# SwiGLU on a 256 MiB input: groups of four rows per partition, whole 64 KiB stores

## Chip, cores and metric

The kernel runs on one core of a Trainium2 chip. The metric is device time in microseconds (us), lower is better. Before the change it is 935.98 us, the median of 3 runs (935.96 to 936.5).

## The reference

```python
def reference(x):                       # x: float32 [8192, 8192]
    a, b = np.split(x, 2, axis=-1)
    silu_b = b / (1 + np.exp(-b))
    return a * silu_b                   # float32 [8192, 4096]
```

Each row of 8192 numbers has its `a` in the first half and its `b` in the second. The input has 268.44 MB, the output 134.22 MB; each number is read or written once, and there is one activation and one product for each output.

## The kernel before, in words

All data stays float32. The 128 partitions of the on-chip memory (SBUF) each take `R = 2` neighbouring rows, so that a tile is 256 rows: 64 KiB in a row of each partition, 8.39 MB in all, and there are 32 tiles. Three slots of 64 KiB per partition (line 39) hold tile i in slot i modulo 3.

The work on a tile is four steps, each in place:

- `load` (line 54): one DMA from `x` into the slot, issued on SyncE's queue (SP). In the view `xv` the two rows of a partition are contiguous, so one partition's share is one piece of 64 KiB, and the whole tile is one contiguous stretch of the input.
- the gate (line 66): ScalarE (ACT) replaces the two `b` halves by their SiLU.
- the product (line 70): VectorE (DVE) multiplies `a` by the gate and packs the two products into the first 32 KiB of the slot's partition.
- `store` (line 75): one DMA of these 32 KiB per partition to `out`. Its queue is ACT's, for odd tiles 3 to 23 GpSimd's (POOL), and for the last two tiles SP's.

The order is written by hand: the program runs under `manual_schedule`, so each engine executes in the order of the loop from line 87. Waits come from the data, and `follows_from_others` (line 44) declares which of them are already implied. What matters for the change: load i+3 goes into the slot of tile i and waits for the store of tile i; it stands on SP right after that tile (line 104). Three loads are issued ahead (line 85).

The ends are cut finer: tiles 0, 1 and 2 compute row by row (`swiglu(i, k, k + 1)`), the first store goes out as 4 KiB and 28 KiB per partition (lines 91 and 92), the last load comes in two halves of 32 KiB per partition (lines 106 and 107), and the last tile is computed as one row and two half rows and is stored in two halves (lines 109 to 112).

Of the kernel before, what the change touches and what calls it, by code (L numbers as in the profile page):

```python
# [1 line left out]

# [4 lines left out]

_SILU = mybir.ActivationFunctionType.Silu


@with_exitstack
def kernel(
    ctx: ExitStack,
    tc: tile.TileContext,
    x: bass.AP,
    out: bass.AP,
):

    nc = tc.nc
    N, M = x.shape
    half = M // 2
    P = nc.NUM_PARTITIONS
    R = 2
    BUFS = 3  # L30

    xv = x.tensor.reshape([N // R, R * M]).ap()
    ov = out.tensor.reshape([N // R, R * half]).ap()
    ntiles = N // (P * R)
    last = ntiles - 1

    pool = ctx.enter_context(tc.tile_pool(name="sbuf", bufs=1))
    ctx.enter_context(tc.manual_schedule())
    slots = [pool.tile([P, R * M], x.dtype, name=f"slot{s}") for s in range(BUFS)]
    loads, gates, prods, stores = ([[] for _ in range(ntiles)] for _ in range(4))  # L40

    newest = {}

    def follows_from_others(inst, i, current, earlier):


        targets = [t for kind in current for t in kind[i]]
        targets += [t for kind in earlier for j in range(i % BUFS, i, BUFS) for t in kind[j]]
        for t in targets:
            if t is not newest.get(inst.ins.engine):  # L50
                tc.declare_no_dep(inst.ins, t.ins, reason="ordered by the other waits")
        newest[inst.ins.engine] = inst

    def load(i, c0=0, cw=R * M):
        inst = nc.sync.dma_start(  # L55
            out=slots[i % BUFS][:, c0 : c0 + cw], in_=xv[i * P : (i + 1) * P, c0 : c0 + cw]
        )
        follows_from_others(inst, i, [], [loads, gates, prods])
        loads[i].append(inst)

    def swiglu(i, k0=0, k1=R, c0=0, cw=half, gated=None):
        rows = slots[i % BUFS].rearrange("p (k s c) -> p k s c", k=R, s=2)
        a = rows[:, k0:k1, 0, c0 : c0 + cw]
        b = rows[:, k0:k1, 1, c0 : c0 + cw]
        o = slots[i % BUFS][:, : R * half].rearrange("p (k c) -> p k c", k=R)
        gate = nc.scalar.activation(out=b, in_=b, func=_SILU)  # L66
        follows_from_others(gate, i, [], [loads, gates, prods, stores])
        if gated:
            gated()
        prod = nc.vector.tensor_mul(out=o[:, k0:k1, c0 : c0 + cw], in0=a, in1=b)  # L70
        follows_from_others(prod, i, [loads], [loads, gates, prods, stores])
        gates[i].append(gate)
        prods[i].append(prod)

    def store(i, c0=0, cw=R * half):
        eng = nc.scalar if i < last - 1 else nc.sync
        if i % 2 and BUFS <= i < ntiles * 3 // 4:
            eng = nc.gpsimd
        inst = eng.dma_start(  # L79
            out=ov[i * P : (i + 1) * P, c0 : c0 + cw], in_=slots[i % BUFS][:, c0 : c0 + cw]  # L80
        )
        follows_from_others(inst, i, [loads, gates], [loads, gates, prods, stores])
        stores[i].append(inst)

    for i in range(BUFS):
        load(i)
    for i in range(last):
        if i == 0:

            swiglu(i, 0, 1)  # L90
            swiglu(i, 1, 2, gated=lambda: store(0, 0, half // 4))
            store(i, half // 4, R * half - half // 4)
        elif i < BUFS:
            for k in range(R):
                swiglu(i, k, k + 1)
            store(i)
        else:
            swiglu(i)
            if i == last - 1:
                swiglu(last, 0, 1)  # L100
            store(i)
        nxt = i + BUFS
        if nxt < last:
            load(nxt)
        elif nxt == last:
            load(last, 0, M)
            load(last, M, M)

    store(last, 0, half)
    for c0 in range(0, half, half // 2):  # L110
        swiglu(last, 1, 2, c0, half // 2)
    store(last, half, half)


# [1 line left out]
_INS = ['x']  # L116
_OUTS = [((8192, 4096), 'float32')]


# [23 lines left out]
```

## Time and profile before

| What | Value |
|---|---|
| Median of 3 runs | 935.98 us |
| Span of the profiled execution (first to last instruction) | 934.2 us |
| VectorE busy | 278.8 us, 30% of the span |
| ScalarE busy | 226.8 us, 24% |
| DMA: bytes and mean rate | 402.67 MB, 431 GB/s |
| Share of the DMA engines' time: SP's queue, ACT's, POOL's | 68.6%, 19.8%, 11.4% |
| A gate and a product of 128 x 8192 outputs | 7.03 us, 8.69 us |
| A gate and a product of 128 x 4096 outputs | 3.61 us, 4.43 us |
| Load, issue to landing (median of 31) | 38.4 us |
| Store of 4096 KB on ACT's queue, issue to landing (median) | 32.8 us |

Busy time of an engine counts its instructions alone, not the issue of DMAs. "Issue to landing" runs from the instruction that starts a transfer to the moment its semaphore is complete, so it holds the time in which the transfer shares the 16 DMA engines with others. The 40 slices of the page give the busy share of each engine in tenths over time; the chain gives the sequence of steps that ended last.

### The profile page before, as it was taken

Reading aid. Unit: us, or ns where it says so; the run is one execution under the profiler, and the core shown is the slowest. Engines: PE = TensorE matmul, PEld = TensorE weight load, DVE = VectorE, ACT = ScalarE, POOL = GpSimd, SP = SyncE. Lnnn points to the kernel's source line nnn. Section 1 sums busy time; section 2 is a strip of 40 time slices with the busy share of each in tenths; the row PEclk is TensorE's granted clock in tenths of the full one; section 3 lists DMA queues with packets and bytes.
Section 4 is the critical chain, followed back from the end, with each engine's and each line's share of the span. In section 5 each row is a group of like instructions: output and inputs, shape, how many; then the busy total and the mean of one; then the engine's idle time right before and its main releaser. Section 6 shows DMA issues by size and latency. Waiting matters only on the chain.

```text
span 934.2 us, 219 instructions
## 1 busy us (share of the span) xinstructions
DVE 278.8 (30%) x37; ACT 226.8 (24%) x38; POOL 6.2 (1%) x15
## 2 busy tenths in 40 slices
DVE  0333123332133321333213333133331233312342
ACT  0412320333202333023330233311333113331141
POOL 0000000000000000000000000000000000000000
DMA  9999999999999999999999999999999999999998
GB/s 404 418 426 434 427 441 450 432 427 429 446 414 441 428 443 431 428 434 459 429 413 460 410 446 428 428 446 427 428 429 464 408 429 446 428 446 428 427 428 382
DMA packets 9649, 402.67 MB, mean 431 GB/s; under 512 B 1072, under 2 KB 1072, under 8 KB 1200
## 3 DMA queue, kind: packets, MB, share of 16 engines
q1 hardware_dynamic: 5184, 276.83, 68.6%
q10 hardware_dynamic: 2880, 79.69, 19.8%
q0 software_dynamic: 1584, 46.14, 11.4%
q14 instruction: 1, 0.01, 0.0%
HBM read 268.44 MB, written 134.22 MB: 431 GB/s over the span
## 4 chain that ended last, share of the span: by engine, by line
DMA 70%; issue 12%; DVE 9%; ACT 7%; DVEq 0%; POOL 0%; SPq 0%; POOLq 0%
DMA slot<-in_x_dram 38%; DMA out_dram<-slot 32%; DVE slot L70 9%; ACT slot L66 7%; DVEq L138 0%; POOL out_dram L79 0%; SPq L55 0%; POOLq L79 0%; DVEq L70 0%
## 5 line engine op out<-in xcount | busy, mean ns | idle before, releaser
L70 DVE TENSOR_TENSOR slot<-slot 128x8192 f32<-128x8192 f32 (+2 forms) x37 | 278.8, 7539 | 641.5 <-ACT slot L66 641.2
L66 ACT ACTIVATE slot<-slot 128x8192 f32<-128x8192 f32 (+2 forms) x37 | 225.5, 6105 | 690.1 <-DMA slot<-in_x_dram 690.1
L79 POOL DMA_DIRECT2D out_dram<-slot x11 | 6.0, 544 | 695.6 <-DVE slot L70 695.6
L66 ACT ACT_TABLE_LOAD x1 | 1.3, 1283 | 0.7 <-PEq L127 0.7
L127 POOL MEMSET const-bfloat16-1.0<- 128x1 bf16 x1 | 0.1, 102 | 0.0
L127 POOL MEMSET const-float32-0.0<- 128x1 f32 x1 | 0.1, 99 | 0.2 <-issue 0.2
L127 POOL MEMSET const-float32-1.0<- 128x1 f32 x1 | 0.1, 99 | 0.0
L127 POOL MEMSET const-uint8-127<- 128x1 uint8 x1 | 0.1, 99 | 0.0
## 6 DMA issues: line engine op xcount, KB each, us to landing
out_dram<-slot ACTq DMA_DIRECT2D x18, 4096.0 KB, 32.8
out_dram<-slot POOLq DMA_DIRECT2D x11, 4096.0 KB, 32.6
slot<-in_x_dram SPq DMA_DIRECT2D x2, 4096.0 KB, 29.8
out_dram<-slot SPq DMA_DIRECT2D x1, 4096.0 KB, 19.3
out_dram<-slot SPq DMA_DIRECT2D x2, 2048.0 KB, 14.5
out_dram<-slot ACTq DMA_DIRECT2D x1, 3584.0 KB, 37.5
out_dram<-slot ACTq DMA_DIRECT2D x1, 512.0 KB, 24.6
slot<-in_x_dram SPq DMA_DIRECT2D x31, 38.4
```

What stands on the lines that cost most here:

```text
L66: gate = nc.scalar.activation(out=b, in_=b, func=_SILU)
L70: prod = nc.vector.tensor_mul(out=o[:, k0:k1, c0 : c0 + cw], in0=a, in1=b)
L79: inst = eng.dma_start(out=ov[i * P : (i + 1) * P, c0 : c0 + cw], in_=slots[i % BUFS][:, c0 : c0 + cw])
L127: nc = _bacc.Bacc("TRN2", target_bir_lowering=False, num_devices=1)
```

## The change

A partition now takes four neighbouring rows (`R = 4`): a group of 512 rows, 128 KiB of input and 64 KiB of output per partition, 16 groups in all. The memory is the same 3 x 64 KiB: two slots called `pack`, used by turns, and one called `extra`.

- The first two rows of a group are loaded into `pack` (h = 0), the last two into `extra` (h = 1). Each load still has 64 KiB per partition, but in `x` each partition's piece now lies 128 KiB from the next partition's.
- The products of `pack`'s two rows are written in place into its first 32 KiB; those of `extra`'s rows into the second 32 KiB of `pack`, whose inputs have been used up by then.
- The store sends the whole `pack`: 64 KiB per partition, one DMA, in ACT's queue, for the last two groups in SP's. The GpSimd queue isn't used.
- The load of `extra` for group g+1 waits for the last product of group g; the load of `pack` for group g+2 waits for the store of group g. They stand on SP in this order.
- The first rows of a group are computed in one gate and one product of 128 x 8192, the last two row by row, in two gates and two products of 128 x 4096.
- The finer cuts at the start and at the end are gone.

The functions `load`, `swiglu` and `store` after the change, and the loop:

```diff
-    R = 2
-    BUFS = 3
+    R = 4
+    W = R * half
...
-    slots = [pool.tile([P, R * M], x.dtype, name=f"slot{s}") for s in range(BUFS)]
+    packs = [pool.tile([P, W], x.dtype, name=f"pack{s}") for s in range(2)]
+    extra = pool.tile([P, W], x.dtype, name="extra")
...
+    def load(eng, g, h, *after):
+        tile_ = extra if h else packs[g % 2]
+        return ordered(
+            eng.dma_start(out=tile_, in_=xv[g * P : (g + 1) * P, h * W : (h + 1) * W]), *after
+        )
...
+    def swiglu(g, h, k0, k1, *after, behind=()):
+        rows = (extra if h else packs[g % 2]).rearrange("p (k s c) -> p k s c", k=2, s=2)
+        o = packs[g % 2].rearrange("p (h k c) -> p h k c", h=2, k=2)
+        b = rows[:, k0:k1, 1, :]
+        gate = ordered(nc.scalar.activation(out=b, in_=b, func=_SILU), *after)
+        return ordered(
+            nc.vector.tensor_mul(out=o[:, h, k0:k1, :], in0=rows[:, k0:k1, 0, :], in1=b),
+            gate, *behind,
         )
...
+    def store(eng, g, c0, c1, *after):
+        return ordered(
+            eng.dma_start(out=ov[g * P : (g + 1) * P, c0:c1], in_=packs[g % 2][:, c0:c1]), *after
+        )
...
-    for i in range(BUFS):
-        load(i)
-    for i in range(last):
...
+    first = {0: load(nc.sync, 0, 0)}
+    second = {0: load(nc.sync, 0, 1)}
+    first[1] = load(nc.sync, 1, 0)
+    for g in range(G):
+        prod = swiglu(g, 0, 0, 2, first[g])
+        prod = swiglu(g, 1, 0, 1, second[g], behind=[prod])
+        prod = swiglu(g, 1, 1, 2, behind=[prod])
+        if g < last:
+            second[g + 1] = load(nc.sync, g + 1, 1, prod)
+        stored = store(nc.sync if g >= last - 1 else nc.scalar, g, 0, W, prod)
+        if g + 2 < G:
+            first[g + 2] = load(nc.sync, g + 2, 0, stored)
```

`ordered` records each instruction and keeps, as its waits, the ones given to it and the order of its own engine.

More of the change, by code (lines that the diff above doesn't have):

```diff
@@ L28 @@
     P = nc.NUM_PARTITIONS
-    R = 2
-    BUFS = 3
+    R = 4
+    W = R * half
     xv = x.tensor.reshape([N // R, R * M]).ap()
-    ov = out.tensor.reshape([N // R, R * half]).ap()
-    ntiles = N // (P * R)
-    last = ntiles - 1
+    ov = out.tensor.reshape([N // R, W]).ap()
+    G = N // (P * R)
+    last = G - 1
     pool = ctx.enter_context(tc.tile_pool(name="sbuf", bufs=1))
     ctx.enter_context(tc.manual_schedule())
-    slots = [pool.tile([P, R * M], x.dtype, name=f"slot{s}") for s in range(BUFS)]
@@ L40 @@
[L40 to L50, printed above, removed]
-                tc.declare_no_dep(inst.ins, t.ins, reason="ordered by the other waits")
-        newest[inst.ins.engine] = inst
@@ L54, in load @@
-    def load(i, c0=0, cw=R * M):
-        inst = nc.sync.dma_start(
-            out=slots[i % BUFS][:, c0 : c0 + cw], in_=xv[i * P : (i + 1) * P, c0 : c0 + cw]
-        )
[L58 to L80, printed above, removed]
-        )
-        follows_from_others(inst, i, [loads, gates], [loads, gates, prods, stores])
-        stores[i].append(inst)
-    for i in range(BUFS):
-        load(i)
-    for i in range(last):
[L88 to L112, printed above, removed]
+    packs = [pool.tile([P, W], x.dtype, name=f"pack{s}") for s in range(2)]
+    extra = pool.tile([P, W], x.dtype, name="extra")
+    ops = []
+    def ordered(inst, *after):
+        before = [t for t in reversed(ops) if t.ins.engine == inst.ins.engine][:1]
+        for t in ops:
+            if not any(t is k for k in [*after, *before]):
+                tc.declare_no_dep(inst.ins, t.ins, reason="ordered by the other waits")
+        ops.append(inst)
+        return inst
```

## The prediction

> **What bounds the kernel now.** I read the page's 40 slices first, then the stretches, then the waits, the forms, the chain and the packet records.
>
> ```profile
> span 934.2 us, 219 instructions
> DVE 278.8 (30%) x37; ACT 226.8 (24%) x38; POOL 6.2 (1%) x15
> DMA  9999999999999999999999999999999999999998
> DMA packets 9649, 402.67 MB, mean 431 GB/s; under 512 B 1072, under 2 KB 1072, under 8 KB 1200
> ```
>
> No compute engine is busy for a third of the span; the DMA engines are busy in all slices. The stretches (length, DVE, ACT and POOL busy, a clock column without meaning here, DMA share, GB/s) show where the rate falls:
>
> ```profile
> 0.00:50.00 50.00, 12.57 (x3) 15.53 (x5) 0.20 (x4) 1.00 1.00 426
> 50.00:60.00 10.00, 5.12 (x2) 0.00 (x0) 0.00 (x0) 1.00 0.94 373
> 60.00:100.00 40.00, 8.85 (x2) 7.12 (x2) 0.00 (x0) 1.00 0.99 428
> 100.00:300.00 200.00, 60.84 (x7) 49.20 (x7) 2.26 (x4) 1.00 1.00 434
> ```
>
> At 434 GB/s the 402.67 MB take 927.8 us, so only 6.4 us of the span could be won by better ordering. ACT waits for loads and SP for stores, which is the same thing seen from the waiting side:
>
> ```profile
> ACT slot L66 <- DMA slot<-in_x_dram: 690.1, 33, 31.1
> SPq L55 <- DMA out_dram<-slot: 866.4, 29, 70.8
> ```
>
> The chain passes load, gate, product, store, load of one slot; one turn is 38.37 + 7.04 + 8.70 + 32.79 = 87 us, three slots share it, so a tile takes 29.0 us (12.58 MB at 434 GB/s). It looks latency-bound but is not: the three turns fill the DMA engines.
>
> ```profile
> 382.27 32.79 DMA out_dram<-slot
> 415.06 0.02 issue
> 415.08 38.37 DMA slot<-in_x_dram
> 453.45 0.02 issue
> 453.48 7.04 ACT slot L66
> 460.51 0.02 issue
> 460.54 8.70 DVE slot L70
> ```
>
> Packet records of the trace (no view prints them one by one; I grouped them by size) give the median time of a packet on its engine: 65,536 B 2.418 us, 32,768 B 1.213, 28,672 B 1.062, 16,384 B 0.611, 4,096 B 0.159, a semaphore write 0.009. Each DMA has 8 packets on each of 16 engines. The first start 1.02 us after the first load's issue, the last ends at 932.9, 1.3 before the span's end.
>
> **What the Trainium skill says.** "DMA: Bandwidth & Descriptors", section "Where 436 GB/s comes from": 435.2 GB/s is the ceiling of the 16 ports. The trace's 434 agrees: nothing is left in steady state. The same page, "Queues, rings and completion order": each DMA engine takes turns between the queues with work, packet by packet. It agrees: a store beside a load lands after 32.8 us, and 7 pairs of 2.418 + 1.213, a last 1.213, 5.9 to the first packet on the last engine (store issued at 440.26, packet records) and 0.3 to the landing make 32.8. The same page, "Issuing engines are not separate DMA queues": the issuer only changes issue time. It agrees: ACT's stores land in 32.8, POOL's in 32.6. The same page, "Latency and other measured facts": a per-partition pitch of 512 KiB gave 207 GB/s against 214 unhindered. No run here shows that.
>
> **The change part by part.** Names: A(g), B(g) the two loads of group g (8.39 MB each, like a load now), S(g) its store.
>
> *Packets.* Per DMA engine, stores of 256 packets' worth of 32 KiB cost 256 x 1.213 = 310.5 us; 128 of 64 KiB cost 128 x 2.418 = 309.5: 1.0 less. The split pieces go too: the last load in halves 16 x 1.213 - 8 x 2.418 = 0.06; the first store, 8 x (0.159 + 1.062 - 1.213) = 0.06; the last, 16 x 0.611 - 8 x 1.213 = 0.07. DMAs fall from 66 to 48, 18 x 0.009 = 0.2. All lies on the bounding resource: **-1.4 us**. I assume that a 64 KiB store packet takes what a 64 KiB load packet takes; both sizes have been bounded by the same 434 GB/s. Below, it can't beat 65,536 B at that ceiling (2.41 us, another 1.1 us); above, two 1.213, which cancels the 1.0.
>
> *Queue of POOL.* 11 stores of 0.53 us issue time leave it, all now on ACT (14) or SP (2). ACT issue takes 0.34 where 0.53 stood; neither bounds: 0. ACT waits for the product with the next A gate behind it, which has no data before A(g+1) lands.
>
> *Compute.* The same elements: 16 products of 8.69 and 32 of 4.43 us make 280.8 against 278.8 us of DVE, gates 16 x 7.03 + 32 x 3.61 = 228 us. DMA hides both. Uncovered, one group costs 7.03 + 8.69 and 12.63 us; the last is today's second tile in the same form, ACT start 42.63 to store issue 55.26.
>
> *Start.* Three whole loads as before. B(0) lands near 42.6, B(1) and S(0) are issued at 42.6 + 12.6 = 55.2, and A(1)'s packets last to 1.8 + 0.8 + 24 x 2.418 = 60.6: 5.4 us of cover, cost 0. Before, the first store was issued at 30.77; with loads queued that makes no difference.
>
> *Steady state, the added waits.* B(g+1) now waits for the product of B(g), as there is one extra slot; A(g+2), behind it in SP's order, waits for S(g). Count from the landing of B(g). The product ends at 12.6; A(g+1) covers it with 19.3 us of packets (8 x 2.418), about 5.3 done, 2.7 left. At 12.6 B(g+1) and S(g) are issued. S(g) alternates with loads, now one to one: 5.9 to the last engine's first packet + 7 x 4.836 + 2.418 + 0.3 = 42.5, landing at 55.1. If nothing idles, B(g+1) lands at 24 x 2.418 = 58.0. A(g+2) therefore has 58.0 - 55.1 = 2.9 us from the landing of S(g) to reach engines that would run dry; it needs 0.05 for the wait and 1.0 from issue to first packet. **Cover 1.8 us, cost 0**, and the period is 58.0, two of today's tiles. That is the thinnest cover in the kernel. The issue latency beside busy engines isn't shown cleanly: 1.0 (queue and engines idle) is the low bound; 4.1 to 5.9 (a new queue beside a busy one) the high one, but this contains packets that the engines had already taken, during which they don't idle. I take 1.0. With 4.1 the shortage is 4.15 - 2.9 = 1.25 us, over 14 handoffs 17.5 us.
>
> *Where loads lie.* A partition reads 64 KiB of every 128 KiB; before, the tile was one piece. Bounds: 0 and the page's (214 - 207) / 214 = 3.3% of the loads' 256 x 2.418 = 619 us, an estimate of 20 us. I take 0: the pitch is a quarter of the page's, the pieces four times longer.
>
> *End.* S(14) stands on SP behind B(15), so all of it (19.3 us) is left to cover the last compute of 12.6; S(15) is issued 6.7 us before S(14) is through, needing 1.0. Then 19.3 us of full-rate store. Cost 0; before, the pieces did the same. What is late next is only the last packet: 2.4 us long instead of 0.6, but each engine has equal work, so the end moves with spread, up to 1 us either way, taken as 0.
>
> *Sum.* 934.2 - 1.4 = 932.8 us of span; the median of runs stands 1.8 above the span, 935.98 - 1.4 = **934.6 us**, a change of 0.15%. A measurement of this kernel can tell about 0.2% (1.9 us) from no change.
>
> **Rivals.** *The slow patch goes.* In 50 to 60 us the rate was 373: 10 x 61 / 434 = 1.4 us lost. The records show 15 loads' packets near 54.5 at 3.1 to 3.2 us instead of 2.42, just as the short first store packets give way to longer ones. Without the split it may vanish: 933.2, faster. Against: the cause isn't visible and whatever a first large store sets off remains.
>
> *The handoff S(g) to A(g+2) starves the engines.* Slower: one mechanism, at each of 14 handoffs. It decides from a loss of 1.8 us beyond my reckoning, one packet's length being 2.4; landings show one DMA engine out of step by a packet (a load's last semaphore write at 424.11, the others by 422.0). From there each missing 0.6 us costs 14 x 0.6 = 8.4: 943.0; at the bound 952. For my side: the lateness of the first packet on the last engine is already counted, and an idle gap gives the next A a later start, so its remainder covers more of the next round.
>
> *The loads' pitch costs.* Half the bound, 10 us: 944.6. Against: each piece is still read in one run of 2.418 us, so a partition changes its address as seldom as before.
>
> *The longer store packets don't pay.* If a 64 KiB store packet takes two of 1.213, the saving falls to 0.4 us: 935.6, still no change.
>
> **How the numbers follow.** Forecast including the last rival: 0.48 (933.9 to 936.5); patch gone: 0.24; starving: 0.20; pitch: 0.08. So faster by over 0.2% (below 934.1) 0.24, within 0.48, slower (above 937.9) 0.28. Cases of both signs flank it, so the forecast's own range is 933.9 to 936.5. The range of 8 in 10 runs from 933.0, the patch case with a little more, to 943.0, the middle of the starving case; left out are about half of that case, half of the pitch case and a little below, some 0.17.
>
> **What would show it.** The page after: DMA 9 in all slices, 434 GB/s in steady stretches, 48 data DMAs, no POOL queue. In the forms A gates start every 58.0 us. In the chain, an SP issue follows a store landing about 2.9 us before the B load lands. Right packets: 65,536 B of the stores at 2.418. Wrong if the period is over 58.3 (starving: DMA share under 1 near each A issue; pitch: load packets longer at full share), or if the stretch 50 to 60 moves at 434.

## The result, and the profile after

| | Before | After |
|---|---|---|
| Median of runs | 935.97 us (4 runs, 935.23 to 936.5) | 965.93 us (4 runs, 964.04 to 971.32) |
| Profiled execution: time, span | 936.0, 934.2 us | 966.08, 964.3 us |

The ratio is 1.0329 (95% interval 1.0302 to 1.0357): slower by 30 us where 934.6 was forecast. Against the forecast span of 932.8 us, 31.5 us have to be found.

The page of the kernel after:

```profile
span 964.3 us, 220 instructions
DVE 279.2 (29%) x48; ACT 227.7 (24%) x49; POOL 0.2 (0%) x4
DMA  9999999999999999999999999999999999999998
DMA packets 6914, 402.67 MB, mean 418 GB/s; under 512 B 768, under 2 KB 768, under 8 KB 768
```

The bytes and the compute are the same, and the DMA engines still show 9 in every slice. Only the mean rate fell, from 431 to 418 GB/s. A slice of 24 us with 9 tenths can't show a gap of a microsecond, nor a packet that takes 4 us instead of 2.4: both count as busy or nearly so. The same stretches as before (length, DVE, ACT and POOL busy, clock, DMA share, GB/s):

```profile
0.00:50.00 50.00, 12.97 (x2) 15.43 (x4) 0.20 (x4) 1.00 0.98 419
50.00:60.00 10.00, 4.48 (x2) 0.00 (x0) 0.00 (x0) 1.00 1.07 419
60.00:100.00 40.00, 8.69 (x1) 7.03 (x1) 0.00 (x0) 1.00 0.97 419
100.00:300.00 200.00, 61.11 (x11) 49.58 (x11) 0.00 (x0) 1.00 1.00 421
```

The loss is not at an end: the steady stretch moves at 421 instead of 434 GB/s, at a DMA share of 1.00. The share does not see it, since a packet counts as busy for its whole length, a stretched one too.

The chain shows the new turn (start, length, what):

```profile
280.62 3.62 ACT extra L63
284.26 8.77 DVE pack L65 x2
293.05 47.82 DMA extra<-in_x_dram
340.89 3.63 ACT extra L63
344.54 8.77 DVE pack L65 x2
353.33 47.35 DMA extra<-in_x_dram
```

One turn runs from the landing of one B to that of the next: 340.89 - 280.62 = 60.27 us; the prediction had 58.0. The mean over 14 groups is 60.0. The same group on the timeline (start, length, engine, line; in brackets the idle time before and its releaser) shows the handoff, the moment at which the landing of S(g) lets SP issue A(g+2):

```profile
293.05 0.33 SPq L55 DMA_DIRECT2D extra<-in_x_dram  x1
293.06 0.36 ACTq L71 DMA_DIRECT2D out_dram<-pack  x1
...
337.19 0.33 SPq L55 DMA_DIRECT2D pack<-in_x_dram  x1
340.89 7.12 ACT L63 ACTIVATE extra<-extra 128x4096 f32<-128x4096 f32 x2 [26.77 <-DMA extra<-in_x_dram]
...
353.33 0.33 SPq L55 DMA_DIRECT2D extra<-in_x_dram  x1
```

The store lands 56.6 us after B's landing (the prediction: 55.1), and A is issued 3.7 us ahead of the landing of the B before it (the prediction: 2.9). Read so, the handoff looks better covered than forecast. What this view can't show is that a landing belongs to the last of 16 DMA engines.

The packet records, grouped by DMA engine, show the rest. (They don't name the engine; each packet is put to the engine whose last packet ended as it began.) In this group the first engine had finished B's packets 1.1 us after A's issue. Over the 14 handoffs B lands 2.4 to 4.9 us after A's issue, but its first engine is through between 0.5 us before and 1.8 us after it. So some engines have no work. The median packet of loads and stores is 2.418 us, as hoped; the mean load packet is 2.515, the longest 4.2. An engine's time beyond the median is 26.3 us over the run, against 1.6 before. It lies in two places: at the handoff, and about 16 us later, where the next store starts.

### The profile page after: what moved, and what is told of

Its sections match the earlier page's. It is cut to its first block, busy times and chain, and to the rows that moved or that the text cites. A ratio compares the mean times of both kernels' runs of the same rounds, so it can differ in the third digit from the quotient of the medians.

```text
span 964.3 us, 220 instructions
## 1 busy us (share of the span) xinstructions
DVE 279.2 (29%) x48; ACT 227.7 (24%) x49; POOL 0.2 (0%) x4
## 4 chain that ended last, share of the span: by engine, by line
DMA 76%; DVE 14%; ACT 6%; DVEq 0%; issue 0%; SPq 0%
DMA extra<-in_x_dram 76%; DVE pack L65 14%; ACT extra L63 6%; DVEq L111 0%; SPq L55 0%
## 5 line engine op out<-in xcount | busy, mean ns | idle before, releaser
L65 DVE TENSOR_TENSOR pack<-pack 128x8192 f32<-128x8192 f32 x16 | 139.1, 8692 | 340.8 <-ACT pack L63 340.8
L65 DVE TENSOR_TENSOR pack<-extra 128x4096 f32<-128x4096 f32 x32 | 140.2, 4421 | 317.2 <-ACT extra L63 317.2
L63 ACT ACTIVATE extra<-extra 128x4096 f32<-128x4096 f32 x32 | 114.0, 3608 | 398.4 <-DMA extra<-in_x_dram 398.4
L63 ACT ACTIVATE pack<-pack 128x8192 f32<-128x8192 f32 x16 | 112.5, 7029 | 305.1 <-DMA pack<-in_x_dram 305.1
```

What stands on the lines that cost most here:

```text
L63: gate = ordered(nc.scalar.activation(out=b, in_=b, func=_SILU), *after)
L65: nc.vector.tensor_mul(out=o[:, h, k0:k1, :], in0=rows[:, k0:k1, 0, :], in1=b),
```

## The experiments

The first theory had two separate bills: a 64 KiB store that starts after a pause disturbs the loads beside it, and each handoff leaves the load queue dry. The rivals were the dry queue alone, the loads' 128 KiB pitch, and the size of the packets. "Dry" below means: some DMA engine has finished all loads issued so far. The kernels whose label begins with m move this kernel's bytes without its arithmetic: they leave out gate and product and store a tile as it was loaded.

### Stores in two halves, and two queues

The store goes out as two column halves, the first already when the first product is ready:

```diff
         prod = swiglu(g, 0, 0, 2, first[g])
+        half_a = store(eng, g, 0, W // 2, prod)
...
+        half_b = store(eng, g, W // 2, W, prod)
...
-            first[g + 2] = load(nc.sync, g + 2, 0, stored)
+            first[g + 2] = load(nc.sync, g + 2, 0, half_a, half_b)
```

> The store of a group goes out in two column halves, each as soon as its products are there, so that some store is in flight nearly all the time and the second half is done long before the next load into the same slot is needed. Theory (two costs at each group of the changed kernel: about 1.2 us when the stores begin after some 20 us with loads alone, about 0.9 us when the load queue runs dry before the store has landed): both go, some 936 us. Rival (the pitch of 128 KiB between partitions slows the loads): the loads are as they were, so it stays near 966. Rival (only the dry queue costs; the long packets at the start of the stores follow from it): 936 as well.

Measured: 938.45 us (937.53 to 938.99), ratio 1.0028 [1.0016, 1.0039]. Nearly all of the loss is gone, with the loads still 64 KiB, so pitch and load packets alone don't make it. But the edit changes three things at once: the stores hardly pause, their packets are 32 KiB, and A's issue comes earlier.

The whole store on two queues, in halves of 64 partitions:

```diff
+            s0 = store(nc.scalar, g, 0, P // 2, prod)
+            s1 = store(nc.gpsimd, g, P // 2, P, prod)
```

> The whole store of a group, 64 KiB packets, goes out at the same moment as in the changed kernel, but as two halves of 64 partitions on two queues, so that it takes two turns in three and lands some 7 us earlier. The load queue no longer runs dry; the time with loads alone gets longer. Theory of two costs: the dry queue's 13 us go, the 16 us at the start of the stores stay, some 952 us. Rival (the dry queue is the cause of everything): 936. Rival (pitch): 966.

Measured: 1034.55 us in the fastest of four runs, 1050.17 to 1064.57 in the others; the profile is of the fastest. Nothing follows for the theories: packets of the 64-partition stores took 2.60 us on average (ACT's queue) and 2.95 (POOL's), the loads' 2.56, and each DMA engine idled 19.7 us in all, so the edit brought larger costs of its own.

### The pitch alone

The loads read contiguous tiles; the rows so come in another order.

```diff
+    xt = x.tensor.reshape([N // 2, W]).ap()
...
-            eng.dma_start(out=tile_, in_=xv[g * P : (g + 1) * P, h * W : (h + 1) * W]), *after
+            eng.dma_start(out=tile_, in_=xt[(2 * g + h) * P : (2 * g + h + 1) * P, :]), *after
```

> Each load reads one contiguous 8 MiB stretch of the input as in the kernel before (so the rows come in another order than the output needs), all else as in the changed kernel. Theory of two costs: no difference, 966 us. Rival (the pitch of the loads): back to some 936 to 950.

Measured: 965.87 us (962.68 to 966.98), ratio 1.0316 [1.0296, 1.0335], the time of the kernel after. The pitch costs nothing that can be measured here.

### The traffic alone: stores without pause, and with it

Two load slots by turns, and a store of a tile that stays in memory. In m0 the next store always stands in ACT's queue; in m8 a store starts at every second load, so that it pauses as in the kernel after, while a load is always queued ahead. m4 and m2 were to have shorter pauses, with DMAs of half and a quarter of the partitions. In the loop of m8, `old` is load j-2, and `look` copies one column on ACT as soon as a load has landed, which sets the pace of the stores.

```python
        loads.append(ordered(nc.sync.dma_start(out=slots[t % 2][s, :], in_=src), *old))
        if j % 2 == 1:
            look(j - 1)
            store(whole)
```

> Traffic alone, no gate and no product: 32 loads of 8 MiB into two slots, always one queued ahead, and 16 whole stores of one loaded tile, each issued when the one before has about landed, so that stores never pause for more than about 5 us until all are out. Same bytes and packets as the changed kernel. Theory (a cost of about 1.2 us each time stores begin after loads alone): one such start, some 934 to 937 us. Rival (mixing 64 KiB stores with loads costs by itself): 950 or more.

> The same traffic, but a store is issued after every second load, so that about 19 us of loads alone lie between two stores (8 packets per DMA engine), 15 times, while the load queue never runs dry. Theory: 15 starts at 1.2 us on top of the run without pauses, some 952 us. Rival (only a dry load queue costs): as without pauses, some 935.

> The same bytes in DMAs of 64 partitions: 31 pauses of about 10 us. If each start of the stores costs 1.2 us whatever the pause: some 970 us. If the cost needs a long pause or is in proportion to it: 952 or less, down to 935.

> The same bytes in DMAs of 32 partitions: 63 pauses of about 5 us, which is what the kernel before has between two stores without any long packet in its trace. Theory with a threshold between 5 and 20 us: some 936 us. If every start costs: over 1000.

Measured: m0 938.97 us (ratio 1.0031 [1.0015, 1.0046]), m8 947.06 (1.0119 [1.0089, 1.0148]), m4 1504.3, m2 1520.19. m4 and m2 say nothing on pauses: with fewer partitions the median load packet takes 4.9 us. m8 refutes the first theory. A 64 KiB store that starts after a pause costs 0.92 us per engine the first time and 0.13 at each later start, not the 1.2 of the kernel after. But m8 is 8 us over m0, for another reason, which is visible at its end (length, ACT and POOL busy, clock, DMA share, GB/s):

```profile
900.00:915.00 15.00, 0.00 (x0) 0.00 (x0) 1.00 1.07 459
915.00:930.00 15.00, 0.00 (x0) 0.00 (x0) 1.00 0.99 428
930.00:945.00 15.00, 0.00 (x0) 0.00 (x0) 1.00 0.32 140
```

In the last 15 us the DMA share is 0.32: by the packet records, eight of the 16 engines end at 931.4 to 931.8, eight run on to between 936.4 and 944.4. They have drifted apart.

### Splitting the wait of A

The load of `pack` in two column halves, each behind the store of its own half. Both store halves still go out together, after the last product, so the stores' pause stays. `extra` gets a gap of 8 elements between its halves, which makes all packets 32 KiB. (`early` is the product of `pack`'s rows; the store half that waits for it stands on ACT behind the half that waits for the last product.)

```diff
-    extra = pool.tile([P, W], x.dtype, name="extra")
+    extra = pool.tile([P, 2, M + 8], x.dtype, name="extra")[:, :, :M]
...
+                eng.dma_start(out=packs[g % 2][:, k * M : (k + 1) * M], in_=xv[r, k * M : (k + 1) * M]),
+                *after[1 - k : 2 - k],
...
+            for k in (1, 0)
...
-        stored = store(nc.sync if g >= last - 1 else nc.scalar, g, 0, W, prod)
+        stored = [store(eng, g, M, W, prod), store(eng, g, 0, M, early)]
```

> The stores begin at the same moment and pause as long (some 20 us) as in the changed kernel, but store and first load of a group go as two column halves, the load of a half waiting for the store of that half alone, and every packet has 32 KiB, so that loads and stores still take turns one to one. The load queue gets its next 32 KiB packets about 20 us before it would run dry. Theory A (two separate costs: 1.2 us at each start of the stores, 0.9 us at each dry queue): about 13 us better than the changed kernel and 2 to 3 us worse for the smaller packets, some 955 us. Theory B (the dry queue is the one cause; the long packets when the stores begin are its second half): 936 to 941 us and no long packets after the first group.

Measured: 937.54 us (20 runs, 937.04 to 937.94), ratio 1.0017 [1.001, 1.0023]. The loss is gone. The timeline:

```profile
287.97 0.38 SPq L56 DMA_DIRECT2D extra<-in_x_dram  x1
287.98 0.91 ACTq L81 DMA_DIRECT2D out_dram<-pack  x2
...
311.76 20.87 SPq L59 DMA_DIRECT2D pack<-in_x_dram  x2
333.68 7.12 ACT L73 ACTIVATE extra<-extra 128x4096 f32<-128x4096 f32 x2 [28.06 <-DMA extra<-in_x_dram]
...
346.12 0.38 SPq L56 DMA_DIRECT2D extra<-in_x_dram  x1
```

The first half of A is issued at 311.76, 21.9 us before B lands at 333.68. When the second half is issued, about 20.5 us after the first, each engine has eight packets of the first half queued, 8 x 1.213 = 9.7 us. The turn is 346.12 - 287.97 = 58.15 us.

### Packets of 32 KiB, waits unchanged

e4 changed two things, so the packet size was tried by itself: `packs` and `extra` both get the gap, and the waits are those of the kernel after.

```diff
-    packs = [pool.tile([P, W], x.dtype, name=f"pack{s}") for s in range(2)]
-    extra = pool.tile([P, W], x.dtype, name="extra")
+    packs = [pool.tile([P, 2, M + 8], x.dtype, name=f"pack{s}")[:, :, :M] for s in range(2)]
+    extra = pool.tile([P, 2, M + 8], x.dtype, name="extra")[:, :, :M]
```

> The changed kernel with nothing altered but the length of the packets: a gap of 32 bytes in the middle of each tile's partition makes each DMA move two pieces of 32 KiB for every one of 64; the waits, the queues and the order of the DMAs stay. Theory D (the load queue runs dry because engines take two packets ahead, and so each handoff is late by packets, not by a fixed time): with packets half as long the first store packet comes about 2.4 us sooner and what is taken ahead is half as long, so the dry queue is cured at most handoffs, 938 to 945 us. Rival (the length of the packets has no part in it, only the waits): 964 to 968 us.

Measured: 962.67 us (962.0 to 963.72), ratio 1.0289 [1.0272, 1.0306]; the expectation missed. Small packets don't cure it. With e4 this is the cleanest pair: packets of 32 KiB in both, a store that starts with B's issue in both, and A's wait differs. (e4 also sends A and the store as two DMAs each. That the cut itself is the cure was not tried apart; in e1 A is one DMA, and the loss is nearly gone too.) Here is one turn of each, cut at the same moments after the store's issue: store start, both kinds, then the handoff (columns as above). First e7, then e4:

```profile
293.00:301.00 8.00, 0.00 (x0) 0.00 (x0) 0.00 (x0) 1.00 0.99 373
301.00:336.00 35.00, 8.69 (x1) 7.03 (x1) 0.00 (x0) 1.00 1.00 433
336.00:346.00 10.00, 1.58 (x1) 5.23 (x2) 0.00 (x0) 1.00 1.00 406
```

```profile
288.00:296.00 8.00, 0.00 (x0) 0.00 (x0) 0.00 (x0) 1.00 1.02 442
296.00:331.00 35.00, 8.69 (x1) 7.03 (x1) 0.00 (x0) 1.00 1.01 434
331.00:341.00 10.00, 3.67 (x1) 7.12 (x2) 0.00 (x0) 1.00 0.99 426
```

Between them the two run alike (433 and 434). At the handoff e7 moves 406 against 426 GB/s, and at the store's start 373 against 442. (Packets are counted where they start, so stretches this short are good to a few per cent.) So one wait, A's, makes both losses, though the second shows 16 us after it.

### The second load in halves, 64 KiB packets kept

B comes in two column halves, each behind the product of its own row of `extra`, and the gates wait for their half. A is then to be issued over 10 us before any engine runs out of loads, and A and the stores keep 64 KiB packets.

```diff
+                eng.dma_start(out=extra[:, k * M : (k + 1) * M], in_=xv[r, W + k * M : W + (k + 1) * M]),
+                *after[k : k + 1],
...
+            for k in range(2)
...
-            second[g + 1] = load(nc.sync, g + 1, 1, prod)
+            second[g + 1] = load(nc.sync, g + 1, 1, row0, prod)
```

> The changed kernel with whole 64 KiB stores and whole first loads, but the second load of a group in two column halves of 32 KiB packets, so that its first row is computed while the second half still comes: the store is issued 8.1 us after the last landing instead of 12.6, and beside 32 KiB load packets it takes two bytes in three. The next first load is then on its queue over 10 us before the load queue would run dry. Theory B: the dry queue is all that was wrong with the change; what remains is the sum of the prediction (934.6 us) plus 128 more packets per engine at 0.008 us, 935 to 937 us, and long packets in the first group alone. If anything else in the change costs (whole stores, the pitch of the loads, the uncut ends): 940 or more.

Measured: 955.13 us (953.91 to 957.26), ratio 1.02 [1.0186, 1.0215]. The queue is never dry, and yet 955, not 937: the expectation missed. As in m8, the engines drift: ten end at 943 to 945, six at 947.7 to 952.4, and the landing of one load spreads over up to 21 us. A is issued 12.2 us before the first engine runs out at the first handoff, but only 1.5 to 5 us before it from the sixth on. Most of the loss is long packets: 14.5 us per engine from S(1) on, about half of it at store starts, which cost 0.05 to 0.38 us from S(1) to S(4) and 0.52 to 1.12 from S(5) to S(13). So a store start can become dear without a dry queue, once the engines are out of step. That 64 KiB packets bring this second loss is suggested by e4, which has none of them and none of it; the pair m8_pause and m8_pause_small below tests it for the drift.

### The dry queue and the packet size, in the traffic alone

m8_dry lets the load queue run dry: the stores send slot 0 itself, so every second load waits for a store. The two "small" kernels are m8_pause and m8_dry with 32 KiB packets.

```diff
-        old = loads[j - 2 : j - 1]
+        old = loads[j - 2 : j - 1] + ([stores[j // 2 - 1]] if j % 2 == 0 and j else [])
```

> Traffic alone, as with the pause of about 20 us, but the store sends the slot of every second load, and the next load into this slot waits for that store, so that the load queue runs dry 15 times, right after the store, some 20 us before the next store begins. It needs some 1.3 us of empty engines each time by construction. Theory A: at the start of the stores the packets stay as short as in the run with the pause alone (0.15 us a time); 947 + 15 x 1.3 to 2.5, so 967 to 985 us. Theory B: besides that, long packets of about 1 us on each engine at the start of the stores, or a longer gap; 980 to 1000 us.

> The traffic with the dry queue and the pause (991 us with 64 KiB packets), with packets of 32 KiB. If a dry queue costs by itself: the long packets at the start of the next stores stay, some 0.9 us per engine a time, 985 to 995 us. If the 64 KiB packets are what makes the start of the stores dear: they go, and only the gap itself stays, 965 to 980 us.

> The traffic with the pause of 20 us and a load queue that never runs dry (947 us with 64 KiB packets, where some DMA engines fell behind the others by up to 25 us), with packets of 32 KiB. If the falling behind comes from 64 KiB packets: all engines end together and 936 to 940 us. If from the pause: 945 to 950 us.

| us | Queue dry | Never dry |
|---|---|---|
| 64 KiB packets | 991.28, ratio 1.059 [1.0568, 1.0611] | 947.06, ratio 1.0119 [1.0089, 1.0148] |
| 32 KiB packets | 993.62, ratio 1.0616 [1.0595, 1.0637] | 937.09, ratio 1.0011 [1.0004, 1.0018] |

At either size the dry queue is by far the larger cost, here with an idle time of 2.3 us at each handoff. The packet records show its second part as well: each later store start has 0.93 us of long packets per engine in m8_dry and 0.85 in m8_dry_small, against 0.13 and 0.02 where the queue is never dry. (The columns differ in more than the wait: the dry kernels send the tile just loaded and have no `look`; both pause some 20 us between stores.) With 32 KiB packets and no dry queue, a pause of the stores costs nothing. The end of that kernel, to be laid beside the one above:

```profile
900.00:915.00 15.00, 0.00 (x0) 0.00 (x0) 1.00 1.02 439
915.00:930.00 15.00, 0.00 (x0) 0.00 (x0) 1.00 0.98 424
930.00:945.00 15.00, 0.00 (x0) 0.00 (x0) 1.00 0.23 100
```

All its engines end between 933.5 and 934.3; most of what the last line holds is the first 4 us of its stretch.

### A shorter step before the store

The gate and product of the group's third row in two halves of 2048 columns, to let S and B start a little earlier:

```diff
-        prod = swiglu(g, 1, 0, 1, second[g], behind=[prod])
+        prod = swiglu(g, 1, 0, 1, second[g], behind=[prod], c1=half // 2)
+        prod = swiglu(g, 1, 0, 1, behind=[prod], c0=half // 2)
```

> The changed kernel with the third row of a group computed in two halves of 2048 columns, so that the store is issued about 1.6 us sooner after the landing of the second load, and the cover of the handoff grows by as much. Theory B (two packets are taken ahead on each engine; the next load has to be there about 3 us before the first engine is through, in the changed kernel it comes 0 to 1.8 us before): the cover becomes some 1.5 to 3.4 us, so a part of the handoffs is cured, 945 to 960 us. Theory A: the same for the dry part, at most 13 us better, 953 to 966.

Measured: 962.91 us (956.2 to 968.91), ratio 1.0285 [1.0232, 1.0337], a little above the 945 to 960 expected. It tells more than its time: some handoffs are now disturbed and some aren't, side by side in one run. Packet records give the long packets and idle time at each handoff, and the long packets at the store start after it, in us per engine:

```
handoff  0     1.03  .53   1.67  0     7.62  0     1.12  .06   .83   1.55  .03   1.39
store    0     1.28  1.72  1.30  .16   1.18  .27   1.48  .26   1.53  .58   .20   1.12
```

Five undisturbed handoffs are followed by 0 to 0.27, eight disturbed ones by 0.58 to 1.72. In the five, A was issued 2.4 us or more before the first engine was through, in the eight at most 1.3 us before it.

## Why the prediction was wrong

All per group and DMA engine, from the packet records (the 14 groups with a handoff, for e4 without the first store start; "no loss" is 24 packets of 2.418, or 48 of 1.213):

| Kernel | Packets | Long at store start | Long at handoff | Idle | No loss | Period |
|---|---|---|---|---|---|---|
| after | 64 KiB | 1.18 | 0.60 | 0.37 | 58.0 | 60.0 |
| e7, waits unchanged | 32 KiB | 0.95 | 0.48 | 0.3 | 58.2 | 59.9 |
| e4, A's wait split | 32 KiB | 0.01 | 0.01 | 0 | 58.2 | 58.2 |

**The step that failed** is the handoff: "it needs 0.05 for the wait and 1.0 from issue to first packet. **Cover 1.8 us, cost 0**". Three things were off in it.

- The cover was counted to the wrong engine. 2.9 us from S's landing to B's landing was near the truth (2.4 to 4.9), but B's landing is the end of its last engine. The first is through 0.9 to 3.1 us earlier.
- The need was taken as 1.0 us, from an idle queue at the program's start. In the contiguous kernel, e3, two handoffs had A issued 3.0 and 4.0 us before the first engine was through. The store starts after them cost 0.25 and 0.00 us instead of 0.9 to 1.7. In the kernel after, with at most 1.8 us, all but one lost 0.2 us or more at once; that one, its first, had 1.7 us and lost 0.03 at the handoff, but 1.01 at the next store start. In e5, 2.4 us were enough. So with engines in step the need lies between 1.8 and 2.4 us, about twice what was assumed.
- The price was taken too low. The bound of 17.5 us was 14 x 1.25, the missing time itself. Measured are 14 x (60.0 - 58.0) = 28 us, about half of it at the next store start, where the prediction put nothing. The records' total is 16.5 (store starts) + 8.3 (handoffs) + 5.0 (idle) = 29.8 us. 0.8 of it stood in the kernel before too, at its first large store; 0.67 for the start of S(14) and 1.4 for the engines' spread at the end come on top. That makes 31.1 of the 31.5 us.

**The rival "starving"** was the right mechanism with the wrong size. Its counterargument, that a gap gives the next A more cover, did not hold in the kernel after: none of its 14 handoffs has cover enough. It held once in e3, where an A that came 5.4 us too late was followed by a cover of 4.0 us, and at several handoffs of e5.

**The rival "slow patch goes"** misread its line. It hoped that the patch would go with the split store; but the first large store sets it off, split or not, as its own counterargument feared. The kernel before pays 0.8 us per engine where its 28 KiB store packets follow the 4 KiB ones, the kernel after 1.03 at its first store, e4 1.09, m8 0.92. A start after a dry load queue costs about as much again; that both are the same thing is not shown.

**Right, by their own measures:** store packets take 2.418 us, so the 1.4 us of packets were saved; with both losses gone, e4 is 934.6 + 16 x 24 x 0.008 for its halved packets = 937.7, and measures 937.54. The pitch costs nothing (e3). Compute stays hidden (DVE 279.2, ACT 227.7 us). B(1) and S(0) go out at 54.51 instead of 55.2. S(15) is issued at 937.26 and the engines end at 959.6 to 963.2, with no gap ahead. One count was off without consequence: the kernel before has 67 DMAs (33 loads, 34 stores), not 66.

**What is shown and what is not.** That the late A makes the loss, the part at the next store start too, rests on e4 against e7 (25.1 us), on the traffic with and without a dry queue (993.62 against 937.09 with 32 KiB packets), and on e5's pairs. Packet size has its share: in the kernel after the three losses sum to 2.15 us, in e7 to 1.73, so 14 x 0.42 = 5.9 us go with the 64 KiB packets; less 3.1 for the halved packets, 2.8 us are left, near the 3.3 that e7 won. The shares don't simply add: e6 kept the queue filled, with 64 KiB packets in A and the stores, and won 11 us, e7 changed the packets alone and won 3, e4 changed both and won 28. Open are three whys: why an engine that has run dry pays again at the next store start, why engines drift apart with 64 KiB packets and pausing stores, and why store starts grow dear in e6 without a dry queue. That each dry handoff brings the engines back into step in the kernel after would fit its narrow end, but was not tried. No version here beats the kernel before; the nearest are m8_pause_small, which computes nothing, at ratio 1.0011 and e4 at 1.0017.

## What to carry to other kernels

When a transfer waits for another's landing and nothing is queued behind it, count the cover to the first DMA engine that runs out, not to the landing, and ask for more than the issue latency: here 1.8 us of queued packets were too few and 2.4 enough. A load that is split by what each part waits for keeps the queue filled at almost no cost in memory: e4 did so with the same three slots, one of them 32 bytes longer per partition. And a busy share of 1.00 proves no full rate: read GB/s by stages, and the spread of packet times.

## What was not expected of the hardware

- The first large store cost 0.77 to 1.15 us per engine in every kernel whose DMAs span 128 partitions; in the kernel before, whose first store packets have 4 KiB, it came only with those of 28 KiB. Where the load queue ran dry before it, each later start cost that again (0.95 in e7 against 0.01 in e4).
- Loads over fewer partitions were slow: in m4, with 64 partitions for each DMA, the median 64 KiB load packet took 4.94 us instead of 2.418, and in m2, with 32, 4.90. Their store packets took 2.6. m4's page:

```profile
span 1512.3 us, 230 instructions
...
DMA packets 7667, 402.68 MB, mean 266 GB/s; under 512 B 1521, under 2 KB 1521, under 8 KB 1521
```

- The Trainium skill, "DMA: Bandwidth & Descriptors", section "Queues, rings and completion order", says that each DMA engine has a ring of its own for each queue. The traces agree, and show what follows: nothing keeps the 16 in step. One load's landing spread over 0.4 us early and 25 us late in m8 with 64 KiB packets; with 32 KiB its engines ended within 0.8 us.
